# The prompt's linear-attention chunks taken two at a time

## The chip, the cores and the metric

One core of a Trainium2 chip runs the program. The core has a matrix engine (TensorE, PE in the profile; its weight loads are PEld), a vector engine (VectorE, DVE), a scalar engine (ScalarE, ACT), a small general engine (GpSimd, POOL) and a queue that issues most transfers (SyncE, SP). Matmuls write into PSUM, eight banks of 128 partitions x 512 float32 values; ACT and DVE read them out into SBUF. The metric is the device time in microseconds of one execution.

## What is computed

The reference is one layer of a decoder trunk for 1024 prompt tokens and 8 x 8 sample tokens (1088 in all, model width 1024). One input projection gives the pooling input `u`, its gate `gp`, queries, keys and values `q`, `k`, `v`, the gate `gg` and a low-rank forget gate. Group A is a causal pooling mixer, group B a gated linear attention (GLA) with four heads, keys of 64 and values of 128. Both are gated, concatenated and mapped by an output projection, and a layer norm ends the layer. What the change touches is the GLA of the prompt, which the reference writes as a recurrence over chunks:

```python
def step(S, inp):
    qb, kb, vb, gb = inp
    b = jnp.cumsum(gb, axis=2)
    inter = jnp.einsum('bhck,bhkv->bhcv', qb * jnp.exp(b), S)
    ...
    A = jnp.einsum('bhtk,bhsk,bhtsk->bhts', qb, kb, decay)
    intra = jnp.einsum('bhts,bhsv->bhtv', A, vb)
    bC = b[:, :, -1]
    S_new = jnp.exp(bC)[..., None] * S + jnp.einsum('bhsk,bhsv->bhkv', kb * jnp.exp(bC[:, :, None] - b), vb)
    return S_new, inter + intra
```

Each head's output is then divided by its root mean square over the 128 values. The kernel uses chunks of 128 tokens (eight for the prompt; chunk 8 is the sample) and folds the decay into K and Q when they are written, so that a chunk needs five kinds of matmul: keys turned (a transpose), scores (K by Q), a state product (turned keys by values), and two parts of the output (old state by Q, values by masked scores).

## The kernel before

Class `Body` writes the program twice: a fast form, and a `safe` form behind a flag, which these inputs don't take. Within the fast form the order of the code is the order on each engine.

**Projections.** Weights lie in the array, tokens stream past, in three token chunks of 384, 384 and 320. One call of `group(i, c)` (L370) makes one output block of 128 columns for one token chunk: 24 matmuls, since every float32 product is made as three products of split halves (`mm3`, L66: L68, L69, L70). Order: the k and q blocks (i = 0 to 3), then u (4 to 7), gp (8 to 11), gg (12 to 15). The result `psm` lies in one of two banks of the pool `psp`; ACT or DVE takes it out.

**What sets the order.** After each group `tick` (L85) runs the pieces of other work that have come due; a call of `tick` is a slot. `later(d, fn)` (L82) puts a piece d slots ahead, and pieces of one slot run in the order of their numbers. For u blocks, `pool_steps` (L632) first takes `psm` out, and after the tick its `chain` writes sums over windows, their difference to the input and its split (`pdhl`) on DVE; the map product `psmap` with it on PE (L675) comes two slots later. A new weight block is split into halves (`hl`) by ACT and DVE in each slot with c = 0.

**GLA.** `gla_steps(c)` (L683) gives the pieces of chunk c: `s1a` turns its keys (`pskt`, L725); `s2p` makes the state products (`psp_`, L774); `s1b` makes the scores (L741) into the second half of the bank of `pskt` and into a second bank `psa1`, then ACT copies the turned keys (`kt`, L732) and DVE masks the scores (`am`, L745); `s2` makes the output from the old state (L810) and from the masked scores (L812), into the second half of the bank of `psp_` and into `pso1`, then DVE updates the state `S` (L788, L793, L794), ACT squares the output (L832), and the squares are split; `s3` sums the squares with a matrix of ones on PE (`psms`, L841), takes the root by a logarithm and an exponential on ACT (L845, L846; L844 loads their table where the gate's function had replaced it), and DVE multiplies the output by it into a new page `vm` (L852). All these tiles of PSUM come from the pool `psg` of six banks. The numbers at L439 put keys and scores of chunk c, state and output of chunk c-1 into one slot, so PE has one burst every second slot from slot 0 on, and `s3` one slot behind the output.

PE's array is divided differently for the kinds, as the profile's shapes show: 128*128 for projections, transposes, masked outputs and norm sums; 64*128 (two row halves) for scores and old-state outputs; 128*64 (two column halves) for state products.

Of the kernel before, what the change touches and what calls it, by code (L numbers as in the profile page):

```python
# [7 lines left out]
F32 = mybir.dt.float32  # L8
FR = mybir.dt.float32r
# [11 lines left out]
NB = 8  # L21
# [18 lines left out]
class Body:  # L40
# [54 lines left out]
    def emit(self):  # L95
# [587 lines left out]
    def gla_steps(self, c):  # L683
# [16 lines left out]
        def s0k():  # L700
            if not self.safe:
                kd = gl.tile([128, 2, n], F32, tag="khl", bufs=1, name="kd")
# [27 lines left out]
        def keys():  # L730
            kt = self.kt8 if sample else gl.tile([128, 256], F32, tag="kt", bufs=1 if self.safe else 2, name="kt")
            nc.scalar.activation(kt[:n], st["pa"][2][:n, :256], AF.Copy)  # L732
            st["kt"] = kt

        def s1b():
# [11 lines left out]
            if sample:  # L747
                qb = gl.tile([128, 2, NB, 4, SEG], F32, tag="shl", bufs=1, name="qb")
# [7 lines left out]
        def sample_inter():  # L756
# [9 lines left out]
            st["in"] = gl.tile([128, 512], F32, tag="sin", bufs=1, name="sin")  # L766
            nc.scalar.activation(st["in"], ps, AF.Copy)

        def s2p():
            v, kt = self.v[c], st["kt"]  # L770
            pp = st["pp"] = g_tile("psp_")
            for h in range(4):
                p = h // 2
                nc.tensor.matmul(pp[rows[h % 2], p * 128:(p + 1) * 128], kt[:, h * 64:(h + 1) * 64], v[:, h],  # L774
                                 start=True, stop=True)
            old = st["S"] = self.S
            sn = old if self.safe and c > 0 else gl.tile([128, 2, 128], F32, tag="S", bufs=1 if self.safe else 2, name="S")
            st["sn"] = sn

        def decay():  # L780
            sn, old = st["sn"], st["S"]
            ppv = st["pp"][:, :256].rearrange("k (p v) -> k p v", p=2)
            db = self.dec[:, :, c:c + 1].broadcast_to([128, 2, 128])
            if c == 0:
                if self.safe:
                    nc.vector.tensor_copy(sn, ppv)
                else:
                    nc.vector.tensor_tensor(sn, ppv, db, op=ALU.mult)  # L788
            elif self.safe:
                nc.vector.tensor_tensor(sn, old, db, op=ALU.mult)  # L790
                nc.vector.tensor_tensor(sn, sn, ppv, op=ALU.add)
            else:
                nc.vector.tensor_tensor(sn, ppv, old, op=ALU.add)  # L793
                nc.vector.tensor_tensor(sn, sn, db, op=ALU.mult)  # L794
# [4 lines left out]
        def s2():  # L799
            v, am, kt = self.v[c], st["am"], st["kt"]  # L800
            if not sample:
                if self.safe:
                    s2p()

                po = [st["pp"][:, 256:], g_tile("pso1")]
                dst = [po[h % 2][:, h // 2 * 128:h // 2 * 128 + 128] for h in range(4)]
                if c > 0:
                    for h in range(4):
                        p, r = h // 2, rows[h % 2]
                        nc.tensor.matmul(dst[h], st["S"][r, p], st["Qi"][r, p], start=p == 0, stop=False)  # L810
                for h in range(4):
                    nc.tensor.matmul(dst[h], v[:, h], am[:, h], start=c == 0, stop=c == 0 or h >= 2)  # L812
                decay()
# [51 lines left out]
        return [s1, s2, s3] if self.safe else [s1a, s1b, s2p, s2, s3]  # L865
# [176 lines left out]
```

## Time and profile before

| | |
|---|---|
| time, median of 3 runs | 394.59 us (394.2 to 394.87) |
| the profiled execution's own time | 395.04 us |
| its span, first to last instruction | 393.1 us |
| granted TensorE clock, mean | 0.993 |
| PE busy | 382.5 us, 97% |
| DVE busy | 217.4 us, 55% |
| ACT busy | 144.4 us, 37% |
| transfers | 34.29 MB, 87 GB/s mean |

The page gives each engine's busy time, the chain of work that ended last, and groups of instructions by line of the kernel. In a row of the timeline stand start and duration in microseconds, the engine, the line, the operation, and output<-inputs with their shapes; "x8" is eight records. A float32 product of GLA shows as two records, a transpose or a product of split halves as one. [...]

### The profile page before, as it was taken

The page shows a single profiled execution, that of the slowest core. Times are in us where ns is not written, and L with a number is a line of the kernel's source. Part 1 is how long each engine was busy: PE and PEld are TensorE (multiplying, and loading weights), DVE is VectorE, ACT ScalarE, POOL GpSimd, SP SyncE. Part 2 cuts the span into 40 slices and gives each one's busy share as a digit, 9 for nine tenths or more (in the row PEclk, how much of TensorE's full clock was granted, in tenths as well). Part 3 has the DMA queues.
Part 4 walks back from the last instruction along what each step waited for, and adds up shares of the span by engine and source line. Part 5 has one row for each costly group of instructions (what it writes and reads, how often), then busy time and mean ns, then how long its engine had stood idle before and what let it go on. Part 6 is the DMA issues. An engine that isn't in the chain of part 4 may idle for free.

```text
span 393.1 us, 6078 instructions
## 1 busy us (share of the span) xinstructions
PE 382.5 (97%) x2473; PEld 357.5 (91%) x2473; DVE 217.4 (55%) x429; ACT 144.4 (37%) x273; POOL 8.3 (2%) x31
## 2 busy tenths in 40 slices
PE   8999999999999999999999999999999999999990
PEld 7999999999999999999999999999988888788790
DVE  4775555521354768788433321333499466555783
ACT  5554454510024434534766223312381432201200
POOL 1000000000000001000001000100000000000000
PEclk9999999999999999999999999999999999999997
DMA  8970101011110101040102110444331243352411
GB/s 252 377 266 3 29 27 55 5 50 53 55 35 21 53 2 53 2 162 0 56 3 95 55 53 0 163 160 153 117 108 54 99 173 104 108 160 80 135 53 61
DMA packets 11556, 34.29 MB, mean 87 GB/s; under 512 B 1776, under 2 KB 3232, under 8 KB 11264
## 3 DMA queue, kind: packets, MB, share of 16 engines
q1 hardware_dynamic: 10960, 32.24, 24.0%
q0 software_dynamic: 416, 1.46, 1.1%
q8 instruction: 21, 0.34, 0.4%
q10 hardware_dynamic: 144, 0.14, 0.1%
q14 instruction: 15, 0.12, 0.1%
HBM read 27.91 MB, written 5.91 MB: 86 GB/s over the span
## 4 chain that ended last, share of the span: by engine, by line
PE 96%; DVE 1%; DMA 1%; ACT 0%; issue 0%
PE psm L68 16%; PE psm L69 16%; PE psm L70 16%; PE pso L68 7%; PE pso L69 7%; PE pso L70 7%; PE psv L70 4%; PE psv L68 4%; PE psv L69 4%; PE pskt L741 1%; PE psms L841 1%; PE pso L75 1%; PE pso L78 1%; PE pso L812 1%; DMA raw<-wv_dram 1%; PE pss L603 1%
## 5 line engine op out<-in xcount | busy, mean ns | idle before, releaser
L68 PE MATMUL psm<-xc,hl 128*128 128x384 f32 (+1 forms) x384 | 126.0, 328 | 0.0
L70 PE MATMUL psm<-xc,hl 128*128 128x384 f32 (+1 forms) x384 | 125.3, 326 | 0.0
L69 PE MATMUL psm<-xc,hl 128*128 128x384 f32 (+1 forms) x384 | 125.2, 326 | 0.0
L68 PEld LDWEIGHTS psm<-xc,hl 128*128 128x128 f32 x384 | 72.1, 188 | 0.7 <-issue 0.2
L69 PEld LDWEIGHTS psm<-xc,hl 128*128 128x128 f32 x384 | 72.1, 188 | 0.1
L70 PEld LDWEIGHTS psm<-xc,hl 128*128 128x128 f32 x384 | 72.1, 188 | 0.0
L68 PE MATMUL psv<-wv,xc 128*128 128x264 f32 x128 | 36.7, 287 | 0.0
L70 PE MATMUL psv<-wv,xc 128*128 128x264 f32 x128 | 36.5, 285 | 0.1
L69 PE MATMUL psv<-wv,xc 128*128 128x264 f32 x128 | 36.3, 284 | 0.0
L68 PE MATMUL pso<-wo,mx 128*128 128x512 f32 (+1 forms) x85 | 32.0, 377 | 0.0
L69 PE MATMUL pso<-wo,mx 128*128 128x512 f32 (+1 forms) x85 | 32.0, 377 | 0.0
L70 PE MATMUL pso<-wo,mx 128*128 128x512 f32 (+1 forms) x85 | 32.0, 376 | 0.0
L540 ACT ACTIVATE mv<-mv,eps 128x1 f32<-128x1 f32 (+1 forms) x9 | 2.7, 295 | 64.9 <-DVE mv L539 64.9
L404 DVE SCALAR_TENSOR_TENSOR vm<-sg,vecs,vm 128x128 f32<-128x128 f32 (+1 forms) x36 | 10.3, 340 | 27.7 <-ACT sg L398 27.7
L64 DVE TENSOR_TENSOR hl<-raw,hl 128x1024 fp32r<-128x1024 f32 x19 | 23.2, 1223 | 3.8 <-ACT hl L61 3.5
L68 PEld LDWEIGHTS psv<-wv,xc 128*128 128x128 f32 x128 | 24.1, 189 | 0.5 <-ACT xc L61 0.5
L533 DVE SCALAR_TENSOR_TENSOR hh<-xr,pso 128x512 f32<-128x512 f32 (+2 forms) x19 | 12.4, 654 | 22.0 <-PE pso L70 21.8
L645 ACT ACTIVATE ue<-psm 128x384 f32<-128x384 f32 (+1 forms) x12 | 5.5, 456 | 51.9 <-PE psm L70 47.9
L70 PEld LDWEIGHTS psv<-wv,xc 128*128 128x128 f32 x128 | 24.0, 188 | 0.4 <-DVE xc L64 0.3
L69 PEld LDWEIGHTS psv<-wv,xc 128*128 128x128 f32 x128 | 24.1, 188 | 0.0
L61 ACT ACTIVATE hl<-raw 128x1024 fp32r<-128x1024 f32 x19 | 19.9, 1050 | 6.4 <-PE psm L70 6.4
L68 PE MATMUL pso<-hl,mx 128*128 128x512 f32 (+1 forms) x51 | 19.3, 379 | 0.0
(236 smaller groups left out, 586.8 us busy)
## 6 DMA issues: line engine op xcount, KB each, us to landing
raw<-wm_dram SPq DMA_DIRECT2D x16, 512.0 KB, 3.5
xr<-x_dram SPq DMA_DIRECT2D x8, 512.0 KB, 4.3
o_y_dram<-hh SPq DMA_DIRECT2D x7, 512.0 KB, 2.9
wr<-w_out_dram SPq DMA_DIRECT2D x5, 512.0 KB, 4.5
s<-s_dram SPq DMA_DIRECT2D x2, 1024.0 KB, 6.3
hl<-xt_dram SPq DMA_DIRECT2D x2, 768.0 KB, 7.0
raw<-w_out_dram SPq DMA_DIRECT2D x3, 512.0 KB, 3.5
hl<-xt_dram SPq DMA_DIRECT2D x2, 640.0 KB, 5.0
```

What stands on the lines that cost most here:

```text
L61: self.nc.scalar.activation(hi.bitcast(FR), raw, AF.Copy)
L64: (on_lo or self.nc.vector).tensor_tensor(lo.bitcast(FR), raw, hi, op=ALU.subtract)
L68: nc.tensor.matmul(ps, ahi.bitcast(FR), bhi.bitcast(FR), start=first, stop=False)
L69: nc.tensor.matmul(ps, ahi.bitcast(FR), blo.bitcast(FR), start=False, stop=False)
L70: nc.tensor.matmul(ps, alo.bitcast(FR), bhi.bitcast(FR), start=False, stop=last)
L75: one = lambda st, sp: nc.tensor.matmul(ps, both.bitcast(FR), bhi.bitcast(FR), start=st, stop=sp)
L78: nc.tensor.matmul(ps[:64], both[:, :64].bitcast(FR), blo.bitcast(FR), start=False, stop=False)
L404: nc.vector.scalar_tensor_tensor(pg, sg[:, to:to + tn], self.norm[:, m:m + 1], pg, op0=ALU.mult, op1=ALU.mult)
L533: nc.vector.scalar_tensor_tensor(hh[:n, s], x[:n, s], ALPHA if n == 128 else 1.0, ps[h][:n, :wd], op0=ALU.mult, op1=ALU.add)
L603: nc.tensor.matmul(pp[q][64 * h:64 * h + 64, b * 128:(b + 1) * 128], self.km[r, 4 * q + b, hd * 64:(hd + 1) * 64], self.v8[r, hd], start=T ...
L645: nc.scalar.activation(ue[:, HIST:HIST + np_], src[:, :np_], AF.Copy)
L741: nc.tensor.matmul(pa[h % 2][:n, p * n:(p + 1) * n], K[r, p], Q[r, p], start=True, stop=True)
```

## The change

In the fast form the chunks of the prompt are taken in pairs by a new function `gla_pair(j)`, which gives two pieces. `burst` of pair j writes, in this order: four transposes, into one bank of their own, and one ACT copy of it; the scores of both new chunks, into two banks; the output of the two chunks of the pair before, old state first and then masked scores, into two banks; masks on DVE; the state products of the new pair, into one bank; two state updates in a row; squares and splits of the pair before. `finish` makes norm sums and the scaling of the pair before. Burst j runs in slot 4j, finish in slot 4j + 2, five bursts in all (the first without an output, the last with nothing else). States are kept by chunk (`self.before`, three buffers of `S`). Masked scores `am` and turned keys `kt` have one buffer of double size in place of two; some buffers of the sample's chunk share other tags. The safe form keeps its old steps, and the times of the sample's chunk (`AT8`) are the same.

```diff
@@ -430,15 +430,20 @@
         self.glp = self.pool("gl", 1)
         self.ptp = self.pool("pt", 2, "right")
         self.S = None
-        for c in range(9):
-            steps = self.gla_steps(c)
-
-
-            at = AT8
-            if c < 8:
-                at = [2 * c, 2 * c + 1, 2 * c + 3] if safe else [2 * c - .9, 2 * c - .7, 2 * c + 1.2, 2 * c + 1.4, 2 * c + 3]
-            for w, step in zip(at, steps):
-                self.later(w, step)
+        if safe:
+            for c in range(8):
+                for w, step in zip([2 * c, 2 * c + 1, 2 * c + 3], self.gla_steps(c)):
+                    self.later(w, step)
+        else:
+
+            self.before = {}
+            for j in range(5):
+                burst, finish = self.gla_pair(j)
+                self.later(4 * j - .5, burst)
+                if j > 0:
+                    self.later(4 * j + 1.6, finish)
+        for w, step in zip(AT8, self.gla_steps(8)):
+            self.later(w, step)
...
-            am = gl.tile([128, 4, 128], F32, tag="am", bufs=1 if self.safe else 2, name="am")
+            am = gl.tile([128, 4, 128], F32, tag="am", bufs=1, name="am")
...
-        return [s1, s2, s3] if self.safe else [s1a, s1b, s2p, s2, s3]
+        return [s1, s2, s3]
...
+    def gla_pair(self, j):
+        nc, gl = self.nc, self.glp
+        new, old = [2 * j, 2 * j + 1] if j < 4 else [], [2 * j - 2, 2 * j - 1] if j > 0 else []
+        rows = [slice(0, 64), slice(64, 128)]
+        st = {}
+        tok = lambda c: slice(128 * c, 128 * c + 128)
+        col = lambda i, p: slice(256 * i + 128 * p, 256 * i + 128 * p + 128)
+        def g_tile(name):
+            return self.psg.tile([128, 512], F32, tag="g", name=name)
+        def burst():
+            if new:
+                pk, pa, pp = g_tile("pskt"), [g_tile(f"psa{e}") for e in range(2)], g_tile("psst")
+                for i, c in enumerate(new):
+                    for p in range(2):
+                        nc.tensor.transpose(pk[:, col(i, p)], self.K[:, p, tok(c)], self.ident)
+                kt = gl.tile([128, 2, 256], F32, tag="kt", bufs=1, name="kt")
+                nc.scalar.activation(kt.rearrange("t i c -> t (i c)"), pk, AF.Copy)
+                for i, c in enumerate(new):
+                    for h in range(4):
+                        r, p = rows[h % 2], h // 2
+                        nc.tensor.matmul(pa[h % 2][:, col(i, p)], self.K[r, p, tok(c)], self.Q[r, p, tok(c)],
+                                         start=True, stop=True)
+            if old:
+                po = st["po"] = [g_tile(f"pso{e}") for e in range(2)]
+                opened = [False, False]
+                for i, c in enumerate(old):
+                    for h in range(4):
+                        r, p, e = rows[h % 2], h // 2, h % 2
+                        if c > 0:
+                            nc.tensor.matmul(po[e][:, col(i, p)], self.before[c][r, p], self.Q[r, p, tok(c)],
+                                             start=not opened[e], stop=False)
+                            opened[e] = True
+                for i, c in enumerate(old):
+                    for h in range(4):
+                        p, e = h // 2, h % 2
+                        nc.tensor.matmul(po[e][:, col(i, p)], self.v[c][:, h], self.am[c][:, h],
+                                         start=not opened[e], stop=i == 1 and p == 1)
+                        opened[e] = True
+            if new:
+                am = gl.tile([128, 2, 4, 128], F32, tag="am", bufs=1, name="am")
+                for e in range(2):
+                    for i in range(2):
+                        nc.vector.tensor_tensor(am[:, i, e::2], pa[e][:, 256 * i:256 * i + 256].rearrange("s (p t) -> s p t", p=2),
+                                                self.mask.unsqueeze(1).broadcast_to([128, 2, 128]), op=ALU.mult)
+                self.am = {c: am[:, i] for i, c in enumerate(new)}
+                for i, c in enumerate(new):
+                    for h in range(4):
+                        nc.tensor.matmul(pp[rows[h % 2], col(i, h // 2)], kt[:, i, h * 64:(h + 1) * 64], self.v[c][:, h],
+                                         start=True, stop=True)
+                for i, c in enumerate(new):
+                    sn = gl.tile([128, 2, 128], F32, tag="S", bufs=3, name="S")
+                    ppv = pp[:, 256 * i:256 * i + 256].rearrange("k (p v) -> k p v", p=2)
+                    db = self.dec[:, :, c:c + 1].broadcast_to([128, 2, 128])
+                    if c == 0:
+                        nc.vector.tensor_tensor(sn, ppv, db, op=ALU.mult)
+                    else:
+                        nc.vector.tensor_tensor(sn, ppv, self.before[c], op=ALU.add)
+                        nc.vector.tensor_tensor(sn, sn, db, op=ALU.mult)
+                    self.before[c + 1] = sn
+                    if c == 7:
+                        nc.gpsimd.dma_start(self.io["o_sp"], sn)
+            if old:
+                sq = gl.tile([128, 2, 2, 256], F32, tag="rs", bufs=1, name="sq")
+                hl = st["hl"] = gl.tile([128, 2, 2, 512], F32, tag="sqhl", bufs=1, name="sqhl")
+                for e in range(2):
+                    nc.scalar.activation(sq[:, :, e], po[e].rearrange("v (i x) -> v i x", i=2), AF.Square)
+                for i in range(2):
+                    self.split(hl[:, 0, i], hl[:, 1, i], sq[:, i].rearrange("v e x -> v (e x)"))
+        def finish():
+            rs = gl.tile([128, 2, 512], F32, tag="rs", bufs=1, name="rs")
+            if old[0] >= 4:
+                nc.scalar.preload_act_table_set(EXP_LN)
+            for i in range(2):
+                pm = g_tile("psms")
+                for a in range(2):
+                    nc.tensor.matmul(pm, self.ones.bitcast(FR), st["hl"][:, a, i].bitcast(FR), start=a == 0, stop=a == 1)
+                nc.scalar.activation(rs[:, i], pm, AF.Ln, bias=self.eps[:, 0:1])
+            nc.scalar.activation(rs, rs, AF.Exp, scale=-0.5)
+            for i, c in enumerate(old):
+                page = self.vmp.tile([128, 4, 128], F32, tag="vm", name="vm")
+                for e in range(2):
+                    half = slice(256 * i, 256 * i + 256)
+                    nc.vector.tensor_tensor(page[:, e::2], st["po"][e][:, half].rearrange("v (p t) -> v p t", p=2),
+                                            rs[:, i, 256 * e:256 * e + 256].rearrange("v (p t) -> v p t", p=2),
+                                            op=ALU.mult)
+                self.v[c] = page
+        return burst, finish
```

How it moves the order, first on PE, at a burst in the middle of the stage (`pskt` turned keys, `psa` scores, `pso` and `psp_` outputs, `psst` and `psp_` state products, `psmap` the pooling map that follows). Before, chunk 3's keys and scores with chunk 2's state and output:

```order
L725 MATMUL pskt<-ident,K 128x128 x2
L774 MATMUL psp__1594<-vm,kt 64x128 x4
L741 MATMUL pskt<-Q,K 128x128
L741 MATMUL psa_1600<-Q,K 128x128
...
L810 MATMUL psp__1594<-Q,S 128x128
L810 MATMUL pso_1609<-Q,S 128x128
...
L812 MATMUL psp__1594<-am,vm 128x128
L812 MATMUL pso_1609<-am,vm 128x128
...
L68 MATMUL psmap<-pdhl,wmap 128x384
```

Of the change, pair 2's keys, scores and state with pair 1's output:

```order
L881 MATMUL pskt<-ident,K 128x128 x4
L887 MATMUL psa_1702<-Q,K 128x128
L887 MATMUL psa_1703<-Q,K 128x128
...
L897 MATMUL pso_1719<-Q,S 128x128
L897 MATMUL pso_1720<-Q,S 128x128
...
L903 MATMUL pso_1719<-am,vm 128x128
L903 MATMUL pso_1720<-am,vm 128x128
...
L915 MATMUL psst<-vm,kt 64x128 x8
L68 MATMUL psmap<-pdhl,wmap 128x384
```

Each kind now stands once per pair with twice its matmuls, and the state products have moved from between transposes and scores to the end of the burst.

On DVE, the same place and the pooling chain behind it (`am` masks, `S` state, `sqhl` split squares, `ws` window sums, `pd` difference, `pdhl` its split, for the map on PE). Before, one chunk's work ahead of a chain:

```order
L745 TENSOR_TENSOR am<-pskt,mask 128x2x128
L745 TENSOR_TENSOR am<-psa_1466,mask 128x2x128
L793 TENSOR_TENSOR S<-psp__1460,S 128x256
L794 TENSOR_TENSOR S<-S,dec 128x256
L64 TENSOR_TENSOR sqhl<-sq,sqhl 128x512
L659 TENSOR_TENSOR ws<-ue 128x398
L659 TENSOR_TENSOR ws<-ws 128x396
L665 SCALAR_TENSOR_TENSOR pd<-ws,ue 128x384
L63 CAST pdhl<-pd 128x384
```

Of the change, ahead of the same chain:

```order
L910 TENSOR_TENSOR am<-psa_1440,mask 128x2x128 x2
L910 TENSOR_TENSOR am<-psa_1441,mask 128x2x128 x2
L924 TENSOR_TENSOR S<-psst,S 128x256
L925 TENSOR_TENSOR S<-S,dec 128x256
L924 TENSOR_TENSOR S<-psst,S 128x256
L925 TENSOR_TENSOR S<-S,dec 128x256
L64 TENSOR_TENSOR sqhl<-sq,sqhl 128x512 x2
L664 TENSOR_TENSOR ws<-ue 128x398
L664 TENSOR_TENSOR ws<-ws 128x396
L670 SCALAR_TENSOR_TENSOR pd<-ws,ue 128x384
L63 CAST pdhl<-pd 128x384
```

The block ahead of the chain has ten operations of a pair in place of five of a chunk, in every fourth slot in place of every second.

More of the change, by code (lines that the diff above doesn't have):

```diff
@@ L730, in keys @@
         def keys():
-            kt = self.kt8 if sample else gl.tile([128, 256], F32, tag="kt", bufs=1 if self.safe else 2, name="kt")
+            kt = self.kt8 if sample else gl.tile([128, 256], F32, tag="kt", bufs=1, name="kt")
             nc.scalar.activation(kt[:n], st["pa"][2][:n, :256], AF.Copy)
@@ L747, in s1b @@
             if sample:
-                qb = gl.tile([128, 2, NB, 4, SEG], F32, tag="shl", bufs=1, name="qb")
+                qb = gl.tile([128, 2, NB, 4, SEG], F32, tag="sqhl", bufs=1, name="qb")
                 nc.gpsimd.memset(qb, 0.0)
@@ L765, in sample_inter, with state @@
                                      start=True, stop=True)
-            st["in"] = gl.tile([128, 512], F32, tag="sin", bufs=1, name="sin")
+            st["in"] = gl.tile([128, 512], F32, tag="rs", bufs=1, name="sin")
             nc.scalar.activation(st["in"], ps, AF.Copy)
-        def s2p():
+        def state():
             v, kt = self.v[c], st["kt"]
-            pp = st["pp"] = g_tile("psp_")
+            pp = g_tile("psp_")
             for h in range(4):
@@ L775, in s2p, with decay @@
                                  start=True, stop=True)
[L776 to L783, printed above, removed]
-            if c == 0:
[L785 to L790, printed above, removed]
+            return pp
+        def decay(pp):
+            sn = self.S if c > 0 else gl.tile([128, 2, 128], F32, tag="S", bufs=1, name="S")
+            ppv = pp[:, :256].rearrange("k (p v) -> k p v", p=2)
+            if c == 0:
+                nc.vector.tensor_copy(sn, ppv)
+            else:
+                nc.vector.tensor_tensor(sn, sn, self.dec[:, :, c:c + 1].broadcast_to([128, 2, 128]), op=ALU.mult)
                 nc.vector.tensor_tensor(sn, sn, ppv, op=ALU.add)
-            else:
-                nc.vector.tensor_tensor(sn, ppv, old, op=ALU.add)
-                nc.vector.tensor_tensor(sn, sn, db, op=ALU.mult)
             self.S = sn
@@ L801, in s2 @@
             if not sample:
-                if self.safe:
-                    s2p()
-                po = [st["pp"][:, 256:], g_tile("pso1")]
+                pp = state()
+                po = [pp[:, 256:], g_tile("pso1")]
                 dst = [po[h % 2][:, h // 2 * 128:h // 2 * 128 + 128] for h in range(4)]
@@ L809, in s2 @@
                         p, r = h // 2, rows[h % 2]
-                        nc.tensor.matmul(dst[h], st["S"][r, p], st["Qi"][r, p], start=p == 0, stop=False)
+                        nc.tensor.matmul(dst[h], self.S[r, p], st["Qi"][r, p], start=p == 0, stop=False)
                 for h in range(4):
                     nc.tensor.matmul(dst[h], v[:, h], am[:, h], start=c == 0, stop=c == 0 or h >= 2)
-                decay()
+                decay(pp)
             else:
@@ L864, in gla_steps @@
             return [s0, s0k, s1, sample_inter, s2, s3]
-        return [s1, s2, s3] if self.safe else [s1a, s1b, s2p, s2, s3]
+        return [s1, s2, s3]
[54 more added lines that the diff above has]
+                        nc.vector.tensor_tensor(sn, ppv, db, op=ALU.mult)
+                    else:
+                        nc.vector.tensor_tensor(sn, ppv, self.before[c], op=ALU.add)
[29 more added lines that the diff above has]
+        return burst, finish
```

2 lines of the change are left out of this document (1 added, 1 removed).

## The prediction

> **What bounds the kernel now.** I read the page first: busy times, then the chain that ended last.
>
> ```profile
> span 393.1 us, 6078 instructions
> PE 382.5 (97%) x2473; PEld 357.5 (91%) x2473; DVE 217.4 (55%) x429; ACT 144.4 (37%) x273; POOL 8.3 (2%) x31
> PE 96%; DVE 1%; DMA 1%; ACT 0%; issue 0%
> ```
>
> TensorE (PE) sets the end: 97% busy, and 96% of the chain is its own work. Then the whole stage that the change touches (110 to 215 us, as one row of the view by windows: length, then busy time and instruction count of PE, weight loads, DVE, ACT, POOL), and the list of PE's waits:
>
> ```profile
> 110.00:215.00 105.00, 105.00 (x751) 100.03 (x750) 69.21 (x151) 52.51 (x95) 5.92 (x18) 1.00 0.13 45
> PE psw L190 <- POOL warm L181: 1.0, 1, 1.0
> ```
>
> In these 105 us PE is never idle, its clock is 1.00, and its only wait in the program is one at the start. So there is no stall here to remove. Time can be won only if the same matmuls take less of PE, and lost if PE now has to wait. For the first I read the timeline of PE, record by record. Chunk 3's burst (start, duration, engine, line, output<-inputs):
>
> ```profile
> 151.97 0.31 PE L68 MATMUL psm<-xc,hl 128*128 128x320 f32 x1
> ...
> 155.35 0.31 PE L70 MATMUL psm<-xc,hl 128*128 128x320 f32 x1
> 155.49 0.38 PE L725 MATMUL pskt<-ident,K 128*128 128x128 f32 x2
> 155.81 0.66 PE L774 MATMUL psp__1737<-vm,kt 128*64 128x128 f32 x8
> 156.39 0.37 PE L741 MATMUL pskt<-Q,K 64*128 64x128 f32 x1
> ...
> 156.83 0.27 PE L741 MATMUL pskt<-Q,K 64*128 64x128 f32 x1
> ...
> 156.94 0.27 PE L810 MATMUL psp__1737<-Q,S 64*128 64x128 f32 x1
> ...
> 157.48 0.49 PE L812 MATMUL psp__1737<-am,vm 128*128 128x128 f32 x2
> 157.81 0.39 PE L812 MATMUL pso<-am,vm 128*128 128x128 f32 x2
> 158.03 0.39 PE L812 MATMUL psp__1737<-am,vm 128*128 128x128 f32 x2
> ...
> 158.40 0.42 PE L68 MATMUL psmap<-pdhl,wmap 128*128 128x384 f32 x1
> 158.66 0.34 PE L69 MATMUL psmap<-pdhl,wmap 128*128 128x384 f32 x1
> 158.83 0.34 PE L70 MATMUL psmap<-pdhl,wmap 128*128 128x384 f32 x1
> ...
> 159.55 0.33 PE L68 MATMUL psm<-xc,hl 128*128 128x384 f32 x1
> ...
> 163.19 0.62 PE L841 MATMUL psms<-sqhl,ones 128*128 128x512 f32 x2
> 163.65 0.34 PE L68 MATMUL psmap<-pdhl,wmap 128*128 128x384 f32 x1
> ```
>
> The distance between starts is what a matmul costs PE; the recorded durations overlap. Steady distances: 0.147 us for a 320-wide projection matmul (24 from 151.97 to 155.49), 0.173 for a 384-wide one (21 from 159.55 to 163.19), 0.23 for a norm sum (two from 163.19 to 163.65); 0.11 for two records on the two row halves of the array (156.83 to 156.94, shape 64*128); 0.225 for one product on the full array with its two records (157.81 to 158.03), so 0.11 for a transpose, which has one. The column halves (128*64) I take as the row halves, 0.11 per two records. The burst's work is then 2 transposes 0.22, state 4 x 0.11 = 0.44, scores 0.44, old-state outputs 0.44, masked outputs 4 x 0.225 = 0.90: 2.44. The burst takes from 155.50 (155.35 + 0.147) to 158.40, plus 0.09 by which the first projection after it (0.26) exceeds 0.173: 2.99. The other 0.55 lies where the division of the array changes: full to column halves, to row halves, to full. Three crossings.
>
> The same for chunk 0 (full, rows, full) and chunk 7 (full, columns, rows, full):
>
> ```profile
> 109.94 0.34 PE L70 MATMUL psm<-xc,hl 128*128 128x384 f32 x1
> 110.11 0.38 PE L725 MATMUL pskt<-ident,K 128*128 128x128 f32 x2
> ...
> 111.07 0.44 PE L68 MATMUL psm<-xc,hl 128*128 128x384 f32 x1
> 111.35 0.34 PE L69 MATMUL psm<-xc,hl 128*128 128x384 f32 x1
> ...
> 204.24 0.34 PE L70 MATMUL psm<-xc,hl 128*128 128x384 f32 x1
> 204.51 0.66 PE L774 MATMUL psp__2246<-vm,kt 128*64 128x128 f32 x8
> ...
> 206.65 0.39 PE L68 MATMUL psm<-xc,hl 128*128 128x320 f32 x1
> 206.88 0.31 PE L69 MATMUL psm<-xc,hl 128*128 128x320 f32 x1
> ```
>
> Chunk 0: 110.11 to 111.07 plus an excess of 0.107 (0.28 - 0.173) is 1.06; its work 0.22 + 0.44; so 0.40 for two crossings. Chunk 7: 204.41 to 206.65 plus 0.083 is 2.32; work 0.44 + 0.44 + 0.90; so 0.54 for three. Both say about 0.18 to 0.20 us a crossing.
>
> **The change, part by part.**
>
> *Matmuls.* None is added or removed: 16 transposes, 32 score products, 28 old-state, 32 masked, 32 state, 16 for the norm. Their 0.11 and 0.225 stay. What changes is how often the division changes. Before: chunk 0 twice, and three times in each of eight later bursts (state and outputs of chunk c-1 with keys and scores of chunk c): 26 crossings, 0.40 + 7 x 0.55 + 0.54 = 4.79 us. After: burst 0 full, rows, columns, full: 3. Bursts 1 to 3: transposes full, scores and old-state outputs on rows, masked outputs full, state on columns, full: 4 each. Burst 4 (outputs only): 2. Together 17.
>
> Of these, full-to-row and row-to-full cost 0.40 a pair (chunk 0): one full-to-row in burst 0 (0.20), three pairs in bursts 1 to 3 (1.20), one in burst 4 (0.40) make 1.80. Eight more the trace shows only in part or not at all: full-to-column (three), column-to-full (four), row-to-column (one). From below: full-to-column has a visible gap of 0.10 (204.41 to 204.51), the others might be free: 0.30 in all, total 2.10, saving 2.7. From above: full-to-column and column-to-row cost 0.55 - 0.20 = 0.35 together, and if each of the eight cost all of that, 2.80, total 4.60, saving 0.2. I take half of 0.35 each, 0.175, since the kinds that are seen cost 0.20 and these two together 0.35: 1.40, total 3.20, **saving 4.79 - 3.20 = 1.6 us**.
>
> [...]
>
> *The key copy (L883).* One ACT copy of 128x512 in place of two of 128x256. In burst 0 it stands between the transposes and the state products with only the scores as cover. Rows of ACT (the eviction in front of it in the queue, and a copy of this size out of PSUM):
>
> ```profile
> 110.31 0.49 ACT L645 ACTIVATE ue<-psm 128x384 f32<-128x384 f32 x1 [26.41 <-PE psm L70]
> L767 ACT ACTIVATE sin<-psin 128x512 f32<-128x512 f32 x1 | 0.6, 600 | 0.6 <-PE psin L763 0.6
> ```
>
> The copy can start at 110.80 and be done at 111.40. PE reaches the state products at 110.11 + 0.44 + 0.20 + 0.88 = 111.63. Cover 0.2 us: cost nothing, but thin. In bursts 1 to 3 another 2.2 us (burst 1) or more of output products lie between: no wait. Without cover each late microsecond would be one of the end's.
>
> *DVE.* Same elements, in larger lumps: a pair's masks, state updates and splits stand in one block ahead of the pooling chain of the same slot, whose result PE wants two slots later. Rows:
>
> ```profile
> L745 DVE TENSOR_TENSOR am<-pskt,mask 128x256 f32<-128x256 f32 x8 | 3.4, 422 | 9.3 <-ACT kt L732 9.3
> L794 DVE TENSOR_TENSOR S<-S,dec 128x256 f32<-128x256 f32 x7 | 3.0, 425 | 0.2
> L64 DVE TENSOR_TENSOR sqhl<-sq,sqhl 128x512 fp32r<-128x512 f32 x8 | 5.5, 693 | 8.6 <-ACT sqhl L61 8.6
> L659 DVE TENSOR_TENSOR ws<-ws 128x396 f32<-128x396 f32 (+5 forms) x18 | 10.7, 595 | 0.6
> L665 DVE SCALAR_TENSOR_TENSOR pd<-ws,ue 128x384 f32<-128x384 f32 (+1 forms) x12 | 6.2, 515 | 0.4
> L63 DVE CAST pdhl<-pd 128x384 fp32r<-128x384 f32 (+1 forms) x12 | 4.2, 352 | 1.1
> ```
>
> The masks now have one buffer, so they start only when the previous pair's masked products are through, 1.1 us before the burst ends; 4 x 0.42 = 1.7 put their end 0.6 past it. From there: 4 state steps 1.7, 2 splits 1.4, chain of the second channel group 2 x 0.60 + 0.52 + 0.35 = 2.1: the high half is ready 5.8 us after the burst. PE in that time: pooling map 0.44, 24 projections of 320 (3.53), map 0.52, 24 of 384 (4.16), norm sums 4 x 0.23 = 0.9: it asks at 9.5. Slack 3.7 us. For pair 2 the chain has one addition and one small operation more, 6.7 against 10.3 (both projections 384 wide). So DVE's edits cost nothing; what hides them is two slots of projections.
>
> *ACT.* A pair's logarithms and exponential stand together, and one table load of 1.28 us fewer goes ahead of them (four become three), off PE's path by the same slots:
>
> ```profile
> L844 ACT ACT_TABLE_LOAD x4 | 5.1, 1283 | 0.1
> L732 ACT ACTIVATE kt<-pskt 128x256 f32<-128x256 f32 (+1 forms) x9 | 3.5, 384 | 6.5 <-PE psa L741 6.4
> ```
>
> *PSUM.* The pair takes all six banks of the pool at once; the map after it takes the key bank (free after the copy), the next the first score bank (free after the masks, 0.6 us after the burst, asked for at 4.0), and the output banks are not asked for until the next burst. Nothing waits. *DMA.* No transfer added or moved but the final state, written from burst 3 instead of chunk 7's burst, earlier.
>
> Sum: 395.04 (the profiled execution, span 393.1) - 1.6 = 393.4. It ran 0.45 above the median of the runs shown, 394.59, so for the median: **393.0 us**.
>
> **Rivals.**
>
> *A, nothing measurable.* The unseen crossings cost near the upper end, 0.3 to 0.35 each: saving 0.2 to 0.6, time 394.0 to 394.4. For it: none of the eight is seen alone, and the column phase with its two crossings is the largest remainder (0.35). Against: chunk 7, which enters the columns from a projection, shows only a 0.10 gap there.
>
> *B, the key copy binds in burst 0.* The cover of 0.2 us is gone if semaphores cost a few tenths: 0.3 to 0.5 lost once, time 393.4. For it: the second row above: that copy was always released by the scores, which lie in its own bank. Against: the new bank holds keys only.
>
> *C, slower: DVE is late.* If the pair's block ran past the slot where PE wants the pooling chain, PE would stop at the map behind the norm sums of bursts 1 and 2. It decides once the block is more than 3.7 us later than I have it, for instance if the splits waited for ACT's squares that long. Two stalls of, say, 2 us less 1.6 gained: 397.0. For it: 69 us of DVE work in 105, and PE idle nowhere to absorb a delay. Against: slack of 3.7 and 3.6. [...]
>
> *D, the change doesn't do what it says.* If the pair's matmuls did not stand together there would be 26 crossings still: 394.6. The order on PE shows them together; I count it with A.
>
> **How the numbers follow.** Forecast 0.62 (392.4 to 393.6), B 0.10, A with D 0.19, C 0.09. A measurement of this kernel can tell about 0.2%, 0.8 us, from no change, so faster means below 393.8: 0.62 + 0.10 = 0.72; same 0.19; slower 0.09. The range takes the bounds of the unseen crossings, savings of 2.7 and 0.2, and 0.1 to 0.2 of spread on the high side: 391.9 to 394.6. It leaves out C and little else.
>
> **What would show it.** PE's timeline of bursts 1 to 3 should read 5.2 us (burst 1) and 5.6 us (2 and 3), against 2 x 2.99 for two chunks before; steady distances unchanged; PE still busy through 110 to 213 us; no new entry in its waits. A gap ahead of the first state product of burst 0 means B; one ahead of a pooling map, released by DVE, means C. The forecast is wrong if the bursts come out at 5.9 or more without a wait (A), or if time changes outside this stage.

## The result and the profile after

| | before | changed |
|---|---|---|
| time, median | 394.86 us (394.2 to 395.33) | 392.81 us (392.6 to 393.27) |
| the profiled execution's own time | 395.04 us | 392.77 us |
| its span | 393.1 us | 391.0 us |
| ratio, 95% interval | | 0.9946 (0.9937 to 0.9956) |

The changed kernel is 2.05 us faster; 393.0 was forecast, with a range of 391.9 to 394.6. The page of the changed kernel, with its span, its busy times and its chain:

```profile
span 391.0 us, 6073 instructions
PE 381.0 (97%) x2473; PEld 357.9 (92%) x2473; DVE 216.7 (55%) x429; ACT 139.0 (36%) x255; POOL 9.2 (2%) x31
PE 97%; DVE 1%; issue 0%; POOL 0%; POOLq 0%
```

PE still sets the end, with as many matmuls as before (2473). Its waits, in full:

```profile
PE psw L190 <- POOL warm L181: 1.0, 1, 1.0
```

And the stage that the change touches, as one row of the view by windows (length, then busy time and count of PE, weight loads, DVE, ACT, POOL, then the granted clock):

```profile
110.00:215.00 105.00, 105.00 (x765) 101.27 (x765) 67.72 (x148) 44.57 (x75) 6.75 (x18) 1.00 0.12 42
```

As before, PE is busy throughout, at clock 1.00, and no wait was removed or added. In the same 105 us it now gets through 765 records in place of 751: the same products follow each other more closely. The timeline of PE shows where. Burst 0, burst 2 and burst 4 (the rows of one kind stand together here, "x16" is sixteen records):

```profile
110.17 0.60 PE L881 MATMUL pskt<-ident,K 128*128 128x128 f32 x4
110.70 1.16 PE L887 MATMUL psa<-Q,K 64*128 64x128 f32 x16
111.79 1.09 PE L915 MATMUL psst<-vm,kt 128*64 128x128 f32 x16
112.81 0.44 PE L68 MATMUL psm<-xc,hl 128*128 128x384 f32 x1
113.09 0.33 PE L69 MATMUL psm<-xc,hl 128*128 128x384 f32 x1
...
153.46 0.60 PE L881 MATMUL pskt<-ident,K 128*128 128x128 f32 x4
153.99 1.16 PE L887 MATMUL psa<-Q,K 64*128 64x128 f32 x16
154.98 1.06 PE L897 MATMUL pso<-Q,S 64*128 64x128 f32 x16
155.97 2.05 PE L903 MATMUL pso<-am,vm 128*128 128x128 f32 x16
157.96 1.09 PE L915 MATMUL psst<-vm,kt 128*64 128x128 f32 x16
158.98 0.44 PE L68 MATMUL psmap<-pdhl,wmap 128*128 128x384 f32 x1
...
201.49 0.34 PE L70 MATMUL psm<-xc,hl 128*128 128x384 f32 x1
201.76 1.16 PE L897 MATMUL pso<-Q,S 64*128 64x128 f32 x16
202.85 2.05 PE L903 MATMUL pso<-am,vm 128*128 128x128 f32 x16
204.66 0.39 PE L68 MATMUL psm<-xc,hl 128*128 128x320 f32 x1
204.89 0.31 PE L69 MATMUL psm<-xc,hl 128*128 128x320 f32 x1
```

Read by starts, as in the prediction, with the first projection's excess added: burst 2 is 158.98 - 153.46 + 0.11 = 5.63 us, of which 4.88 is its products and 0.75 its four crossings. Burst 0 is 112.81 - 110.17 + 0.11 = 2.75, with three crossings for 0.55. Burst 4 is 204.66 - 201.66 + 0.08 = 3.08, with two for 0.40. A part of a single crossing can be read too: the same sixteen score records, with transposes ahead of them both times, cost 0.99 with more row halves behind (153.99 to 154.98) and 1.09 with column halves behind (110.70 to 111.79). These 0.10 us lie ahead of the new division; the rest lies in its first records, as in the prediction's rows, where the first pair of row halves takes 0.22 (156.39 to 156.61) and a later one 0.11.

The clean measure is the stretch from the first turning product of burst 0 to the sample's norm sums, since the start of burst 0 and the last store scatter from one execution to the next. Its last row, of the kernel before and of the changed one:

```profile
242.66 0.40 PE L841 MATMUL psms<-sqhl,ones 128*128 128x256 f32 x2
```

```profile
241.11 0.40 PE L837 MATMUL psms<-sqhl,ones 128*128 128x256 f32 x2
```

Before: 242.66 - 110.11 = 132.55 us. Changed: 241.11 - 110.17 = 130.94. The stretch lost **1.61 us**.

### The profile page after: what moved, and what is told of

Its sections match the earlier page's. It is cut to its first block, busy times and chain, and to the rows that moved or that the text cites. A ratio compares the mean times of both kernels' runs of the same rounds, so it can differ in the third digit from the quotient of the medians.

```text
span 391.0 us, 6073 instructions
## 1 busy us (share of the span) xinstructions
PE 381.0 (97%) x2473; PEld 357.9 (92%) x2473; DVE 216.7 (55%) x429; ACT 139.0 (36%) x255; POOL 9.2 (2%) x31
## 4 chain that ended last, share of the span: by engine, by line
PE 97%; DVE 1%; issue 0%; POOL 0%; POOLq 0%
PE psm L68 16%; PE psm L70 16%; PE psm L69 16%; PE pso L68 7%; PE pso L70 7%; PE pso L69 7%; PE psv L68 4%; PE psv L69 4%; PE psv L70 4%; PE pso L903 2%; PE psa L887 1%; PE psw L190 1%; PE psst L915 1%; PE pso L75 1%; PE psms L944 1%; PE pso L78 1%
## 5 line engine op out<-in xcount | busy, mean ns | idle before, releaser
L64 DVE TENSOR_TENSOR hl<-raw,hl 128x1024 fp32r<-128x1024 f32 x19 | 23.2, 1222 | 3.2 <-ACT hl L61 2.8
L68 PEld LDWEIGHTS psv<-wv,xc 128*128 128x128 f32 x128 | 24.4, 190 | 0.3 <-ACT xc L61 0.3
L69 PEld LDWEIGHTS psv<-wv,xc 128*128 128x128 f32 x128 | 24.4, 191 | 0.0
L70 PEld LDWEIGHTS psv<-wv,xc 128*128 128x128 f32 x128 | 24.2, 189 | 0.1
```

The lines of the kernel that those rows point to most:

```text
L64: (on_lo or self.nc.vector).tensor_tensor(lo.bitcast(FR), raw, hi, op=ALU.subtract)
L68: nc.tensor.matmul(ps, ahi.bitcast(FR), bhi.bitcast(FR), start=first, stop=False)
L69: nc.tensor.matmul(ps, ahi.bitcast(FR), blo.bitcast(FR), start=False, stop=False)
L70: nc.tensor.matmul(ps, alo.bitcast(FR), bhi.bitcast(FR), start=False, stop=last)
```

## The experiments

The theory: PE's time changes by the number of crossings between divisions of its array, at 0.175 to 0.20 us each, and by nothing else. The rivals: PSUM laid out by kind (or the pairs as such) brings the gain; the key copy or VectorE costs something that hides a larger gain. The kernel before took 394.72 to 394.75 us (median) beside these runs. The timed runs came in two batches. The changed kernel ran only in the first, and its 392.87 us is the base for the second too (one chunk to a burst, state products behind the transposes, more work on VectorE); the kernel before differs by 0.03 us between the two. "Stretch" below is the one just defined. Where an edit only moves products, its diff gives the order in words.

### The changed kernel again, and both once more in profile

> The changed kernel once more, beside its variants. Theory 1 (fewer crossings between the divisions of PE's array): 1.6 us of PE time saved in the stage, seen the same in every profile; the measured 2.05 us has another 0.4 to 0.5 us that lies behind the last DVE operation (5.5 us to the end of the span before, 5.0 after), which I hold for scatter of the last store. So 1.6 to 2.1 us below the kernel before here, stage length (first transpose of burst 0 to the sample's norm sum) 130.9 us against 132.6. Theory 2 (PSUM by kind, so that copies and masks no longer wait for one another): same time.

Measured: 392.87 us, ratio 0.9956 (0.9942 to 0.9970); stretch 240.97 - 110.03 = 130.94 us, the same to the hundredth. It is the base of the differences below.

The medians differ by 1.9 to 2.05 us and the stretch by 1.61. From the end of the stretch to VectorE's last operation both kernels take 144.90 us. So what is left over lies ahead of burst 0 or behind VectorE's last operation (the last store's way). Two more profiles were made for that.

> The kernel before, profiled a second time. The medians differ by 1.9 to 2.05 us, while the stretch from the first turned keys to the sample's norm sums differs by 1.61 us (132.55 against 130.94) and the stretch from there to VectorE's last operation by nothing. If the rest is scatter of the last store, this second profile has the stretch at 132.5 to 132.6 again, and from VectorE's last operation to the end of the span 4.7 to 5.0 us, as the changed kernel's profiles have, in place of 5.54. If the change has shortened the end too, it is 5.4 to 5.6 us again.

> The changed kernel, profiled a third time, for the same question: the stretch 130.94 us again, and from VectorE's last operation to the end 4.99 and 4.83 us so far; above 5.2 us here would show that this end scatters as widely in the changed kernel as the difference to be explained.

Measured: before, a stretch of 132.55 us again, burst 0 starting at 110.81 (110.11 in the first profile) and 5.14 us from VectorE's last operation to the end (5.54). Changed: 130.94 again, 110.44, and 4.52 (so far 4.99 and 4.83). The stretch repeats exactly; start and end scatter by up to 0.7 and 0.5 us within one kernel. On the mean of these profiles the ends differ by 0.56 us and the starts by 0.25, in the direction wanted and together more than what is left over; with this scatter it isn't shown to be the change's doing. It stays open.

### Kinds kept by chunk inside the pair

The pairs, the banks by kind and the one key copy stay; only the order on PE goes back to one chunk after the other.

```diff
 transposes of both chunks, key copy
-scores of both; old state of both; masked outputs of both; state products of both
+for g in range(2):
+    scores of chunk g; old state of chunk g; masked outputs of chunk g; state products of chunk g
```

> Pairs, banks, copies and DVE work as in the changed kernel, but on PE, behind the four transposes, each chunk's scores, old-state outputs, masked outputs and state products stand together: 30 crossings in place of 17. Theory 1: bursts 1 to 3 0.55 us longer each, burst 0 0.35 and a wait of 0.1 to 0.2 for the key copy, burst 4 0.40: 2.4 to 2.6 us above the changed kernel, about 0.5 above the kernel before. Theory 2 (the layout of PSUM and the pairs' larger copies bring the gain): equal to the changed kernel.

Measured: 395.37 us, ratio 1.0016 (1.0007 to 1.0025), 2.50 above the changed kernel; stretch 133.48, 2.54 longer. Burst 2 in its timeline:

```profile
155.11 0.72 PE L893 MATMUL psa<-Q,K 64*128 64x128 f32 x8
...
156.20 1.16 PE L906 MATMUL pso<-am,vm 128*128 128x128 f32 x8
157.29 0.66 PE L912 MATMUL psst<-vm,kt 128*64 128x128 f32 x8
157.88 0.71 PE L893 MATMUL psa<-Q,K 64*128 64x128 f32 x8
...
160.06 0.66 PE L912 MATMUL psst<-vm,kt 128*64 128x128 f32 x8
160.64 0.44 PE L68 MATMUL psmap<-pdhl,wmap 128*128 128x384 f32 x1
```

Chunk by chunk the array passes through rows, full and columns twice: seven crossings in the burst where the changed kernel has four. In all there are 30 against 17. The order alone, with the layout untouched, gives back the whole gain and more. PSUM by kind is not what brings it. The small wait for the key copy that was expected in burst 0 came too, too short for the list of waits: the first state products start 0.80 us behind the first scores (110.78 to 111.58), the second ones 0.65 (112.17 to 112.82), and the copy ends at 111.54. That is 0.15 of the 2.54 us.

### One chunk to a burst

The changed function and its banks by kind, but with `new = [j]`, `old = [j - 1]`, nine bursts at slots 2j - 0.5, and half-sized buffers.

```diff
-            for j in range(5):
+            for j in range(9):
...
-        new, old = [2 * j, 2 * j + 1] if j < 4 else [], [2 * j - 2, 2 * j - 1] if j > 0 else []
+        new, old = [j] if j < 8 else [], [j - 1] if j > 0 else []
```

> The changed kernel's function and its PSUM laid out by kind, but one chunk to a burst: nine bursts where the changed kernel has five. Crossings theory: the first burst has 0.55 us of them (three), seven have 0.75 (four, as the changed kernel's bursts 1 to 3), the last 0.40, together 6.2 us, against 3.2 in the changed kernel and 4.79 in the kernel before: 3.0 us above the changed kernel and 1.4 above the kernel before, plus 0.1 to 0.4 if the first burst's state products wait for the key copy, which has only one chunk's scores to lie behind. Rival (the gain is PSUM laid out by kind and the order of the products, not the pairs): within 0.3 us of the changed kernel.

Measured: 397.13 us (396.45 to 397.76), ratio 1.0066 (1.0043 to 1.0088); stretch 133.95, 3.01 longer than the changed kernel's, with no entry for the key copy in PE's list of waits (by starts its first state products are 0.06 late: 0.71 behind the first scores, 110.33 to 111.04, against the 0.65 of the second step in the last experiment, which has no copy to wait for). One of its seven bursts of four crossings:

```profile
132.03 0.38 PE L881 MATMUL pskt<-ident,K 128*128 128x128 f32 x2
...
135.10 0.41 PE L68 MATMUL psmap<-pdhl,wmap 128*128 128x320 f32 x1
```

135.10 - 132.03 + 0.10 = 3.17, less 2.44 of products: 0.73 for half the work, as much as a pair pays. By the stretch the crossings theory, 3.0 above the changed kernel, is right and the rival is out. By the medians the kernel is 4.26 above the changed one: its executions lie at 396.5 and at 397.7, and the profile, of an execution at 396.45, shows 0.8 us of the excess behind VectorE's last operation (5.83 us to the end). Why its executions end so late isn't settled.

### State products ahead of the masked outputs

One crossing fewer in bursts 1 to 3: rows, columns, full, and the projections behind are full as well.

```diff
 old-state outputs of the pair before
+state products of the new pair
 masked outputs of the pair before
 masks on VectorE
-state products of the new pair
```

> In bursts 1 to 3 the new pair's state products stand ahead of the masked outputs: full, rows, columns, full, three crossings instead of four. Theory 1: each of three bursts 0.2 us shorter (5.63 to 5.43 for pairs 2 and 3, 5.17 to 4.97 for pair 1), 0.6 us below the changed kernel; the key copy still has the scores and 0.4 to 0.9 us of old-state outputs as cover, no wait. Theory 2: no difference from the changed kernel, the banks are the same.

Measured: 392.05 us, ratio 0.9930 (0.9916 to 0.9943), 0.82 below the changed kernel; stretch 130.37, 0.57 shorter.

```profile
156.69 1.09 PE L903 MATMUL psst<-vm,kt 128*64 128x128 f32 x16
157.71 2.05 PE L909 MATMUL pso<-am,vm 128*128 128x128 f32 x16
159.52 0.42 PE L68 MATMUL psmap<-pdhl,wmap 128*128 128x384 f32 x1
```

The products are those of the changed kernel; the masked outputs now run on into the map with no crossing (157.71 to 159.52 is 1.81 us for sixteen records, 1.80 by their steady distance). 0.19 us for each of three crossings: the price again, and a kernel faster than both.

### The same, with the last burst joined to the sample's products

Masked outputs first (behind the transposes, both full), then old state, scores and state products, and the sample's transposes and scores moved from slot 18 to the two sides of the last burst (slot 15.5), which `at8` does.

```diff
 transposes, key copy
+masked outputs; old-state outputs
 scores
-old-state outputs; masked outputs
 state products
...
-        for w, step in zip(AT8, self.gla_steps(8)):
+        at8 = [11, 15, 18, 18.1, 18.2, 20, 22, 24] if safe else [11, 15, 15.4, 15.6, 18, 20, 22, 24]
+        for w, step in zip(at8, self.gla_steps(8)):
```

> Masked outputs first (transposes, masked outputs on the full array; then old-state outputs and scores on rows; then state on columns), three crossings in bursts 1 to 3 as in the variant before, and the sample chunk's transposes and scores moved from slot 18 into slot 16, its scores directly behind the last burst's row products, which takes two crossings (0.40 us) away. Theory 1: 1.0 us below the changed kernel. Theory 2: no difference. If a wait of the sample's chunk appears (its key copy and masks come earlier, its query block stays in slot 18) it shows in PE's list of waits.

Measured: 392.11 us, ratio 0.9931 (0.9918 to 0.9945), 0.76 below the changed kernel; stretch 130.13, 0.81 shorter. The bursts 1 to 3 explain 0.57 of it as in the last experiment, so the joined end brought 0.24 where 0.4 had been counted. Its rows show why it isn't all saved:

```profile
201.42 0.38 PE L732 MATMUL pskt<-ident,kd 128*64 128x128 f32 x2
201.64 1.95 PE L896 MATMUL pso<-am,vm 128*128 128x128 f32 x16
203.52 1.16 PE L903 MATMUL pso<-Q,S 64*128 64x128 f32 x16
204.61 0.27 PE L749 MATMUL pskt<-Q,K 64*64 64x64 f32 x1
...
204.99 0.41 PE L68 MATMUL psm<-xc,hl 128*128 128x320 f32 x1
```

The sample's scores stand on quarters (64*64), another division than the row halves ahead of them: 1.09 us for the sixteen row-half records (203.52 to 204.61), as long as where column halves follow (110.70 to 111.79 in the changed kernel) or the full array (201.76 to 202.85). I had counted rows and quarters as one; so the last burst and the sample's products together have three crossings in place of four, not two, and the one saved is about the 0.24 measured. Against the kernel of the last experiment the times don't differ.

### State products behind the transposes

The same count of crossings less three, but nothing of PE left beside the key copy.

```diff
 transposes of the pair, key copy
+state products of the new pair
 scores; old-state outputs; masked outputs
-state products of the new pair
```

> The state products of a pair stand directly behind the turned keys of the same pair, so nothing of PE lies beside the copy of the turned keys. In the changed kernel's first burst the copy was ready 1.28 us after the first turning product's start, and PE is done with these products after about 0.55: PE waits about 0.7 us in each of four bursts, 2.8 to 3.0 us; the three bursts 1 to 3 have a crossing less (state products between full products and row halves), and two 0.2 us each cheaper or dearer: between -0.6 and 0. Cover theory: 2.2 to 3.0 us above the changed kernel, with the wait shown at the line of the state products, ended by ScalarE. Rival (the copy costs PE nothing that counts, because PE's time is only its work and its crossings): 0.6 us below the changed kernel.

Measured: 395.45 us, ratio 1.0017 (1.0008 to 1.0027), 2.58 above the changed kernel; stretch 133.41, 2.47 longer. Its one new wait, from the list of PE's waits:

```profile
PE psst L886 <- ACT kt L883: 2.8, 4, 0.7
```

Four waits of 0.7, 2.8 us in all, less 0.57 for the crossings saved leaves 2.2. The list counts from the recorded ends of the transposes. By starts, the step from the transposes to the next kind takes 1.33 us once and 1.29 three times in place of 0.53, 3.08 more, and less 0.57 that is 2.51 for the 2.47 measured. The copy is not cheap. In the changed kernel it is free because the scores stand in front of it, and exactly such a wait in burst 0 was rival B.

### More work on VectorE: eight and sixteen operations

Multiplications that no output uses, in the blocks of bursts 1 and 2 between the state updates and the splits.

```diff
+            if j in (1, 2):
+                spare = gl.tile([128, 2, 128], F32, tag="spare", bufs=1, name="spare")
+                for _ in range(8):        # 16 in the second kernel
+                    nc.vector.tensor_tensor(spare, self.before[2 * j + 2], self.mask.unsqueeze(1).broadcast_to([128, 2, 128]), op=ALU.mult)
```

> Eight more multiplications of 128x256 on VectorE in the blocks of bursts 1 and 2, about 0.34 to 0.45 us each, 2.7 to 3.6 us in all, behind the masking and ahead of the map's operand. The changed kernel's trace leaves 4.1 us between the operand and PE's asking for it after both bursts: with that slack no change, within 0.3 us of the changed kernel. Rival (VectorE's block is the next bound, the slack is gone): each of the two bursts costs what is added, up to 5 to 7 us above the changed kernel.

> Sixteen of these multiplications in each of the two blocks, 5.4 to 7.2 us. With 4.1 us of slack PE waits 1.3 to 3.1 us at the map's products after each of bursts 1 and 2: 2.6 to 6.2 us above the changed kernel, the wait shown at the map's lines and ended by VectorE. Rival (other work of PE moves up, or VectorE's lateness is hidden further on): within 0.5 us of the changed kernel.

With eight: 393.45 us, ratio 0.9964 (0.9951 to 0.9976), 0.58 above the changed kernel, stretch 131.81, 0.87 longer. The expectation, within 0.3 us of the changed kernel, was missed. VectorE and PE after burst 1 (the burst ends at 135.67 here, 0.57 later than in the changed kernel's profile):

```profile
137.91 3.75 DVE L932 TENSOR_TENSOR spare<-S,mask 128x256 f32<-128x256 f32 x8
...
144.64 0.36 DVE L63 CAST pdhl<-pd 128x384 fp32r<-128x384 f32 x1
145.04 0.56 DVE L64 TENSOR_TENSOR pdhl<-pd,pdhl 128x384 fp32r<-128x384 f32 x1
```

```profile
145.37 0.34 PE L68 MATMUL psmap<-pdhl,wmap 128*128 128x384 f32 x1
145.65 0.44 PE L69 MATMUL psmap<-pdhl,wmap 128*128 128x384 f32 x1
145.93 0.34 PE L70 MATMUL psmap<-pdhl,wmap 128*128 128x384 f32 x1
```

The high half of the map's operand (L63) was in time, at 145.00 for 145.37. The low half (L64) was ready at 145.60 for a product that wanted to start at 145.55: the next two products come 0.28 apart in place of 0.18. I had taken the slack, 4.1 us, at the high half; at the low half, which comes 0.6 later and is wanted only 0.17 later, it is 3.7, and the added 3.7 us (3.75 less the overlap of two rows) uses it up. That costs 0.2 us. After burst 2 the same lateness costs 0.67 us, most of it where a split of a weight block, further back in VectorE's queue, comes late for a projection. So the rival (no slack at all, 5 to 7 us) is out, and the slack is measured at just under 3.7 us.

With sixteen: 403.47 us, ratio 1.0241 (1.0206 to 1.0276), 10.6 above the changed kernel, more than either theory had. PE's waits by VectorE at the norm sums and the map:

```profile
PE psmap L68 <- DVE pdhl L63: 4.0, 2, 2.4
PE psms L948 <- DVE sqhl L64: 1.5, 2, 1.2
```

These are four waits in two stalls. In the timeline the first stall has 1.16 us at the norm sums and 1.65 at the map, the second 0.32 and 2.39. The map was the place foreseen, the norm sums were not. The stretch is 10.56 us longer. By starts: from norm sums to map 4.30 and 4.20 us in place of 0.93, 6.64 in all. The map and the 24 projections behind it take 2.85 more after the first stall, the work behind the second 1.07 more, by operands that are late again. Most of the 2.85 shows in the view by windows of this run (the third column from the end is the granted clock):

```profile
144.00:148.00 4.00, 1.59 (x6) 0.60 (x4) 3.76 (x9) 0.00 (x0) 0.00 (x0) 0.90 0.00 0
148.00:154.00 6.00, 5.60 (x17) 5.29 (x18) 5.59 (x15) 4.12 (x6) 0.11 (x1) 0.50 0.00 0
174.00:179.00 5.00, 2.45 (x11) 1.45 (x9) 4.72 (x11) 0.22 (x1) 0.00 (x0) 1.00 0.00 0
```

The clock fell to half in the first stall, at 147.2 with PE still waiting, and came back at 154.0; in the second stall, about as long, and behind it the clock stayed at 1.00. The fifteen products from 149.49 to 154.18 take 4.69 us in place of 2.60 (15 x 0.173), so 2.09 of the 2.85 is the clock's at least; 0.73 lies in the map's first two products, whose low half was also late. Rival C is thus a real danger of such a change, and a dearer one than I had priced it: the first stall, 3.4 us long, cost 6.2 with what came behind it.

## Why the prediction came out right

*PE is bound by its own work and nothing waits.* Right: the list of waits is unchanged, the clock of the stage 1.00.

*The crossings, 4.79 us before and 3.20 after.* Right, and by its parts. Forecast for burst 1 was 5.2 us, for bursts 2 and 3 5.6; measured 5.17 (135.10 - 130.03 + 0.10), 5.63 and 5.63. The price of the eight unseen crossings, taken as half of 0.35 between bounds of 0.04 and 0.35, is confirmed by burst 0, which has one full-to-row, one row-to-column and one column-to-full for 0.55 together. Five orders of the same products give one line:

| kernel | crossings | stretch, us | against the changed one | per crossing |
|---|---|---|---|---|
| state products ahead of masked outputs | 14 | 130.37 | -0.57 | 0.19 |
| changed | 17 | 130.94 | | |
| before | 26 | 132.55 | +1.61 | 0.18 |
| kinds by chunk in the pair | 30 | 133.48 | +2.54 | 0.20 |
| one chunk to a burst | 33 | 133.95 | +3.01 | 0.19 |

The last two rows hold 0.15 and 0.06 us of a late key copy in burst 0; without it both give 0.18.

That two of them (30 and 33) come out above the kernel before, although they keep the banks by kind and one of them the pairs too, is what sets the cause: the change pays by how it orders the kinds on PE. A change of kind alone, within one division, costs nothing: in the prediction's rows scores run into old-state outputs, with other tiles and other lines, at the steady 0.11 (156.83 to 156.94), and in the kernel with the joined end four transposes run into masked outputs in 0.44 (153.62 to 154.06). What happens inside the array in these 0.19 us no run here shows.

None of the crossings between the kinds of this stage came free, and those to and from column halves cost hardly less than the others: the one to them and the one from them in burst 0 have 0.35 us together (0.55 - 0.20), the two of burst 4, from full to row halves and back, 0.40.

*The saving of 1.6 us.* 1.61 by the stretch. The medians have 1.9 to 2.05. The rest, 0.3 to 0.45 us, lies outside the stretch, in the start and the last store, which scatter by as much; the prediction named "time changes outside this stage" as a sign against it, and this part remains unexplained.

*The key copy costs nothing, cover 0.2 us.* Right. ACT in burst 0 of the changed kernel:

```profile
110.37 0.49 ACT L650 ACTIVATE ue<-psm 128x384 f32<-128x384 f32 x1 [26.41 <-PE psm L70]
110.85 0.60 ACT L883 ACTIVATE kt<-pskt 128x512 f32<-128x512 f32 x1
```

The copy is done at 111.45 and the state products start at 111.79: 0.34 us of cover, thin but enough. Rival B did not come; without the cover it is 0.7 us a burst, four times. Its condition, a few tenths from a copy's end to the product behind it, isn't borne out: where the products did wait for the copy they started 0.05 us behind its end (111.75 to 111.80 with the state products behind the transposes).

*VectorE has 3.7 us to spare.* Right in size, wrong in place. In the changed kernel:

```profile
140.30 0.39 DVE L63 CAST pdhl<-pd 128x384 fp32r<-128x384 f32 x1
140.73 0.56 DVE L64 TENSOR_TENSOR pdhl<-pd,pdhl 128x384 fp32r<-128x384 f32 x1
```

```profile
144.80 0.34 PE L68 MATMUL psmap<-pdhl,wmap 128*128 128x384 f32 x1
144.98 0.34 PE L69 MATMUL psmap<-pdhl,wmap 128*128 128x384 f32 x1
```

The high half is ready at 140.69, 5.6 us after the burst (5.8 forecast), for 144.80: 4.1 us. The low half is ready at 141.29 for 144.98: 3.7. The step looked at the wrong operand. That it still gave 3.7 is luck: its high half was put 0.2 too late on VectorE's side and 0.2 too early on PE's, which together make up the difference between the two halves. The eight added operations found the limit where the low half has it. Rival C did not come because of this slack, and its price, 4 us for two stalls of 2, was too low: with sixteen added operations the clock fell to 0.50 in one of two stalls, and that alone cost at least 2.09 us.

*Nothing measurable (A) and not done (D).* Out: the interval of the ratio ends at 0.9956.

## What to carry to other kernels

Where PE never waits, look at the starts of its small matmuls for gaps at each change of the array's division (0.18 to 0.20 us each here), count the changes, and order the work so that products of one division stand together across chunks, with the full-array kind last if full-array work follows. Before putting products next to each other, see what they were covering: moving the state products up by one place saved 0.57 us, and moving them up to the transposes cost 2.5, because the scores had hidden a copy. Measure the slack of another engine at the last operand that is wanted, not at the first.

## What the hardware showed that was not expected

**The shape in the profile does not tell a crossing.** In the value projections, rows of shape 128*128 and 128*64 alternate (from the timeline of PE of the changed kernel):

```profile
47.80 0.28 PE L75 MATMUL psv<-wv,xc 128*128 128x264 f32 x1
47.92 0.28 PE L78 MATMUL psv<-wv,xc 128*64 128x264 f32 x1
48.05 0.28 PE L75 MATMUL psv<-wv,xc 128*128 128x264 f32 x1
```

They start 0.12 to 0.13 us apart with no gap at any change. So it isn't the narrow shape that costs 0.18 us. Nor does it seem to be the type, split halves here and float32 in the state products: in the kernel with the joined end the sample's two transposes, float32 and 128*64, start 0.17 us behind a 384-wide projection (201.25 to 201.42) and run into full-array products in 0.22 (201.42 to 201.64), two at the steady 0.11. Both of these keep to one half of the columns, while the state products, which do cost it, have one half after the other. Whether this makes the difference isn't shown: no run has the same products in one half alone.

**In one stall the clock fell to half, in another about as long it didn't.** In the run with sixteen added operations two stalls stretched the way from norm sums to map from 0.93 us to 4.30 and 4.20. In the first PE's granted clock fell to 0.50 for 6.8 us (147.2 to 154.0), in the second it stayed at 1.00. The fall cost at least 2.09 us on top of the stall. One of the four executions took 405.84 us where the others took 403.2 to 403.52, with a mean clock of 0.975 where they have 0.983 to 0.985; that would fit a fall in both stalls, but it left no trace. The longest single waits of PE were 1.65 us in the stall where the clock fell, of which 0.5 had passed by then, and 2.39 in the one where it didn't. What decides between the two no run here shows.
